# Writing out the order of VectorE and ScalarE through a gated DeltaNet recurrence, with the transposes of each block's normed output behind the next block's products

## The chip, the core and the metric

The kernel runs on one core of one Trainium2 chip (trn2). The metric is device time in microseconds (us), the median over runs. TensorE (PE in the profile) does matmuls and transposes, VectorE (DVE) element-wise work and reductions, ScalarE (ACT) activations, copies and casts, GpSimd (POOL) a few small operations, and SyncE (SP) issues the transfers.

## What is computed

One residual block over 512 tokens of width 1024: a SwiGLU feed-forward half step, a mixer, and a second feed-forward half step, all in float32, each behind an adaptive RMS norm. The change lies in the mixer. Half of it is latent attention; the other half is a gated delta rule with 4 heads of width 128, whose reference carries a state S from chunk to chunk:

```
def step(state, inp):
    u_c, wk_c, qd_c, kd_c, qk_c, gl_c = inp
    v_new = u_c - einsum('bhck,bhkv->bhcv', wk_c, state)
    o_c = einsum('bhck,bhkv->bhcv', qd_c, state) + einsum('bhcs,bhsv->bhcv', qk_c, v_new)
    state = state * gl_c[..., None, None] + einsum('bhck,bhcv->bhkv', kd_c, v_new)
    return state, o_c
...
o_a = _rms(o_a, gdn_norm_w) * silu(gz)
mixed = concatenate([o_a, o_b], axis=-1)       # o_b: the attention's heads
x = x + g2 * (mixed @ w_out)
```

The kernel walks the 512 tokens in four blocks of 128 (p = 0 to 3), so that the recurrence has three steps that depend on a state.

## The kernel before

Float32 products are made of three passes: a tensor is split into a high part, rounded to fp32r, and a low part that holds the rest, and `mm3` (L468 to L470) multiplies high by high, high by low and low by high. The weights come in tiles of 512 KB (`wr`); ScalarE casts the high part (`wh`, L228) and VectorE subtracts for the low part (`wl`, L229). `wr`, `wh` and `wl` have four buffers each, in rotation, so a tile's cast waits until TensorE has used the tile four places ahead of it, and a load waits until the split four places ahead of it is done.

Eight such tiles hold `w_out`: tiles 1 to 4 for the attention's rows, 5 to 8 for the recurrence's rows. `out_attended` multiplies with tiles 1 to 4 (512 columns, L468 to L470); `out_half` multiplies with 5 to 8 for tokens 0 to 255 (256 columns); `out_rest` multiplies with the same tiles for tokens 256 to 511. Each finished output tile is added into `xT` by VectorE (L2391, L2403, L2414), which frees its PSUM buffer; the buffers of `pa` are three in rotation, those of `pb` five.

The recurrence, block p (`recur`): TensorE multiplies the state with `w` (L1966); VectorE subtracts to get `vn` (L1968); TensorE multiplies the state with q (L1974) and ScalarE scales that into `o`; TensorE multiplies `vn` with `kd` for the next state (L1981) and with `qk` for the output (L1989); VectorE makes the new state `S` (L1986) and adds the output into `o` (L1993). GpSimd makes the decayed state `Sg`.

The block's gated norm (`gated_out`): ScalarE squares `o` into `hn` (L2027), VectorE sums it (`gs`, L2028) and makes `ve` (L2003), GpSimd takes the power -1/2 (`ry`, L214), VectorE scales (`on`, L1475), TensorE transposes four 128x128 pieces (L2012), and for each of four heads VectorE makes `mf` (L2018), ScalarE the high part `mh` (L2020) and VectorE the low part `ml` (L2021). `out_half` reads the results of blocks 0 and 1, `out_rest` those of blocks 2 and 3.

Three first weight tiles of the second feed-forward (`fr`, six transfers of 256 KB, split into `fh` and `fl`) are prepared in the same stretch (`early`).

The order. Each engine works off its instructions in program order. The program is written by generators that are stepped in turn: `fill` holds the `w_out` products, `early` the first feed-forward tiles, `gated` the gated norms, `chain` and `rest` what is left of the solving and the attention. A scheduler then places the instructions of all engines by priorities and estimates of its own, unless `follow` ties an instruction behind another one. In the recurrence, `matmuls_in_order` ties TensorE's instructions alone in the order in which they were written (those of `loosely` excepted); VectorE's and ScalarE's order is left to the scheduler.

## Time and profile before

| | |
|---|---|
| three runs | 1026.66, 1027.6, 1026.34 us, median 1026.66 us |
| profiled execution | 1026.66 us, of which the span is 1024.9 us |
| TensorE busy | 1013.4 us, 99% of the span |
| VectorE, ScalarE, GpSimd busy | 775.8, 500.6, 29.4 us |
| weight loads of TensorE (PEld) | 906.2 us |
| granted TensorE clock | 1.0 of full speed |
| moved from and to HBM | 127.18 MB read, 2.49 MB written |
| the stretch of the change | 609 to 644 us of the span |

The profile is one execution. In the rows of a timeline stand the start in us from the span's beginning, the time that the group takes, engine, line, operation, output and inputs, the number of instructions, and in brackets how long the engine idled ahead of it and what ended that. Matmuls are pipelined: a row's length (0.39 us for a 512-column product) is longer than its distance to the next row (0.23 us), and that distance is the price of one more product. On VectorE and ScalarE too a row overlaps the next one by some hundredths.

### The profile page before, as it was taken

To read this page: it belongs to the slowest core of one execution; us is meant where nothing else is said; L and a number is where in the kernel's file an instruction comes from. 1 tells how busy PE (TensorE), PEld (TensorE's weight loads), DVE (VectorE), ACT (ScalarE), POOL (GpSimd) and SP (SyncE) were. 2 spreads that over 40 slices of the span, in tenths; PEclk is the share of its full clock that TensorE was granted. 3 is DMA by queue.
4 is the path that set the end of the run, shared out by engine and by line. 5 is a ranking of instruction groups with operands and counts; after the bars stand their busy time and mean duration, and the time that the engine had idled before them with its cause. 6 is when DMAs were issued, how large, how long until landed. Compare 5 with 4: busy or idle time off the path is not lost.

```text
span 1024.9 us, 16967 instructions
## 1 busy us (share of the span) xinstructions
PE 1013.4 (99%) x6663; PEld 906.2 (88%) x6663; DVE 775.8 (76%) x1363; ACT 500.6 (49%) x895; POOL 29.4 (3%) x74
## 2 busy tenths in 40 slices
PE   8999999999999999999999999999999999999998
PEld 6788899999887899888888888998999999987887
DVE  4789788887787847879888659677888888788541
ACT  5453455556322235567845465364555555634330
POOL 0000000000100000100000011000000000000000
PEclk9999999999999999999999999999999999999999
DMA  9988234344688835311321121122233434383421
GB/s 328 291 271 263 69 98 116 91 123 114 198 290 303 262 83 167 83 42 42 73 73 47 42 83 49 34 58 87 83 108 99 117 90 123 115 274 91 130 61 31
DMA packets 203773, 130.77 MB, mean 128 GB/s; under 512 B 14241, under 2 KB 188334, under 8 KB 203694
## 3 DMA queue, kind: packets, MB, share of 16 engines
q1 hardware_dynamic: 203694, 129.70, 41.9%
q8 instruction: 52, 0.85, 0.3%
q14 instruction: 27, 0.22, 0.1%
HBM read 127.18 MB, written 2.49 MB: 127 GB/s over the span
## 4 chain that ended last, share of the span: by engine, by line
PE 92%; DVE 5%; DMA 1%; issue 1%; ACT 0%; POOL 0%; SPq 0%; DVEq 0%; POOLq 0%
PE pa L354 17%; PE pa L468 16%; PE pa L469 16%; PE pa L470 16%; PE pb L354 13%; PE pa L1250 1%; PE pb L2188 1%; PE pb L2168 1%; PE pb L1250 1%; PE pb L468 1%; PE pb L469 1%; PE pb L470 1%; DVE wl L229 1%; DMA ar<-in_w_ada 1%; PE pb L1743 1%; PE pb L666 1%
## 5 line engine op out<-in xcount | busy, mean ns | idle before, releaser
L228 ACT CAST wh<-wr 128x1024 fp32r<-128x1024 f32 (+1 forms) x93 | 93.8, 1015 | 160.2 <-PE pa L469 130.6
L269 DVE TENSOR_TENSOR wl<-wr,wh 128x1024 fp32r<-128x1024 f32 x96 | 117.3, 1222 | 54.5 <-ACT wh L273 54.5
L229 DVE TENSOR_TENSOR wl<-wr,wh 128x1024 fp32r<-128x1024 f32 (+1 forms) x93 | 108.8, 1176 | 47.2 <-ACT wh L228 46.3
L468 PE MATMUL pa<-hh,wh 128*128 128x512 f32 (+1 forms) x357 | 137.2, 384 | 0.0
L470 PE MATMUL pa<-hh,wl 128*128 128x512 f32 (+1 forms) x357 | 134.9, 378 | 0.0
L469 PE MATMUL pa<-hl,wh 128*128 128x512 f32 (+1 forms) x357 | 134.7, 377 | 0.0
L468 PE MATMUL pa<-ah,wh 128*128 128x512 f32 (+1 forms) x356 | 132.3, 372 | 0.0
L469 PE MATMUL pa<-al,wh 128*128 128x512 f32 (+1 forms) x356 | 131.1, 368 | 0.0
L470 PE MATMUL pa<-ah,wl 128*128 128x512 f32 (+1 forms) x356 | 130.9, 368 | 0.0
L273 ACT CAST wh<-wr 128x1024 fp32r<-128x1024 f32 x96 | 98.0, 1050 | 18.6 <-PE pa L469 11.2
L468 PEld LDWEIGHTS pa<-ah,wh 128*128 128x128 f32 x356 | 67.1, 188 | 13.4 <-ACT wh L228 2.5
L468 PEld LDWEIGHTS pa<-hh,wh 128*128 128x128 f32 x357 | 67.3, 189 | 13.2 <-issue 1.6
L837 DVE SCALAR_TENSOR_TENSOR aa<-ar,sc,aa 128x512 f32<-128x512 f32 x98 | 73.3, 749 | 6.8 <-DMA ar<-in_w_ada 4.8
L470 PEld LDWEIGHTS pa<-hh,wl 128*128 128x128 f32 x357 | 67.3, 188 | 11.9
L470 PEld LDWEIGHTS pa<-ah,wl 128*128 128x128 f32 x356 | 67.1, 188 | 11.0
L469 PEld LDWEIGHTS pa<-hl,wh 128*128 128x128 f32 x357 | 67.4, 189 | 10.7
L469 PEld LDWEIGHTS pa<-al,wh 128*128 128x128 f32 x356 | 67.1, 189 | 10.8
L354 PE MATMUL pa<-hh,wh 128*128 128x256 f32 x240 | 68.0, 283 | 0.0
L354 PE MATMUL pa<-th,wh 128*128 128x256 f32 x240 | 67.9, 283 | 0.0
L354 PE MATMUL pa<-tl,wh 128*128 128x256 f32 x240 | 67.9, 283 | 0.0
L354 PE MATMUL pa<-th,wl 128*128 128x256 f32 x240 | 67.9, 283 | 0.0
L354 PE MATMUL pa<-hh,wl 128*128 128x256 f32 x240 | 67.9, 283 | 0.0
(481 smaller groups left out, 2482.4 us busy)
## 6 DMA issues: line engine op xcount, KB each, us to landing
wr<-in_ffn_w_in SPq DMA_DIRECT2D x79, 512.0 KB
ar<-in_w_ada SPq DMA_DIRECT2D x96, 256.0 KB
wr<-in_ffn_w_out SPq DMA_DIRECT2D x32, 512.0 KB
ar<-in_w_ada SPq DMA_DIRECT2D x22, 512.0 KB
wr<-in_w_in SPq DMA_DIRECT2D x21, 512.0 KB
wr<-in_ffn_w_out SPq DMA_DIRECT2D x16, 384.0 KB
wr<-in_w_out SPq DMA_DIRECT2D x8, 512.0 KB
wr<-in_ffn_w_in SPq DMA_DIRECT2D x8, 384.0 KB
```

Of the source, the lines that this page charges most:

```text
L228: self.nc.scalar.copy(hi, raw)
L229: self.nc.vector.tensor_tensor(out=lo, in0=raw, in1=hi.bitcast(F32), op=ALU.subtract)
L269: sub = lambda out, x, y: nc.vector.tensor_tensor(out=out, in0=x, in1=y, op=ALU.subtract)
L273: nc.scalar.copy(hi[:, :n], raw[:, :n])
L354: nc.tensor.matmul(z, a[:, j, :], b, start=start and j == 0 and i == 0, stop=j == 3 and i == 2, skip_group_check=not start)
L468: mm(out, wh, xh, start=start, stop=False)
L469: mm(out, wh, xl, start=False, stop=False)
L470: mm(out, wl, xh, start=False, stop=stop)
L666: nc.tensor.matmul(pg[32 * q:32 * q + 32, :256], self.sc[:, kc:kc + 1].to_broadcast([P, 32]), a[kc], start=(e == 0), stop=(e == 1), tile_p ...
L837: nc.vector.scalar_tensor_tensor(out=acc, in0=a, scalar=sc, in1=acc, op0=ALU.mult, op1=ALU.add)
L1250: nc.tensor.matmul(z, a[:, j, :], b, start=start and j == 0 and i == 0, stop=j == 3 and i == 2, skip_group_check=not start)
L1743: nc.tensor.matmul(pa[:, ps], kh[:, ps], x[:, ps], start=True, stop=True)
```

## The change

`matmuls_in_order` becomes `steps_in_order`: it ties TensorE's, VectorE's and ScalarE's instructions of the recurrence in the order in which they are written, each engine for itself. Left out are what `loosely` steps (as before) and, on VectorE and ScalarE, the last block's transposing and scaling together with what is left of `fill`.

`gated_out` yields more often: after the squaring, between the transposes and the scaling, and ahead of the low parts; all four `mf` and `mh` stand ahead of the four `ml`. The loop over p steps it by hand: the norm of block p-1 is scaled (`on`) beside the state's products of block p, and its transposes stand straight behind the products with `qk` of block p, where they stood some products later. The sum, `ve` and power of block p stand between block p-1's `mf`, `mh` and its `ml`.

```diff
@@ -162,17 +162,20 @@
             self.ends[i.engine] = i.name
 
     @contextmanager
-    def matmuls_in_order(self, after=None):
-
-        self.loose = set()
+    def steps_in_order(self):
+
+        self.loose, self.free, last = set(), set(), {}
+        engines = mybir.EngineType.PE, mybir.EngineType.DVE, mybir.EngineType.Activation
         with self.traced() as block:
             yield
         for i in block:
-            if i.engine == mybir.EngineType.PE and i.name not in self.loose:
-                if after:
-                    self.follow(i, after)
-                after = i.name
-        self.last_mm = after
+            if i.engine != engines[0] and i.name in self.free:
+                continue
+            if i.engine in engines and i.name not in self.loose:
+                if i.engine in last:
+                    self.follow(i, last[i.engine])
+                last[i.engine] = i.name
+        self.last_mm = last[mybir.EngineType.PE]
 
     @contextmanager
     def queued(self, engine, after=None):
@@ -1998,7 +2001,10 @@
 
         nc = self.nc
         ss = self.small(4, "gs")
-        self.head_squares(self.o[p], ss)
+        sq = self.slot(s="hn")
+        nc.scalar.activation(sq, self.o[p], AF.Square)
+        yield
+        nc.vector.tensor_reduce(out=ss, in_=sq.rearrange("p (h d) -> p h d", h=4), axis=AX.X, op=ALU.add)
         ve = self.small(4, "ve")
         nc.vector.scalar_tensor_tensor(out=ve, in0=ss, scalar=1.0 / P, in1=self.oe[:, 4 * p:4 * p + 4], op0=ALU.mult,
                                        op1=ALU.add)
@@ -2010,16 +2016,19 @@
         pt = self.aux()
         for h in range(4):
             nc.tensor.transpose(pt[:, h * P:(h + 1) * P], on[:, h * P:(h + 1) * P], self.ident)
+        yield
         m = self.slot(s="mf")
         ts = slice(p * P, (p + 1) * P)
-        for h in range(4):
-            hs = slice(h * P, (h + 1) * P)
-            mh, ml = self.mixed[h]
+        parts = [(slice(h * P, (h + 1) * P), *self.mixed[h]) for h in range(4)]
+        for h, (hs, mh, _) in enumerate(parts):
             nc.vector.scalar_tensor_tensor(out=m[:, hs], in0=pt[:, hs], scalar=self.cwT[:, j:j + 1],
                                            in1=self.zT[h][:, ts], op0=ALU.mult, op1=ALU.mult)
             nc.scalar.copy(mh[:, ts], m[:, hs])
+        yield
+        for hs, mh, ml in parts:
             nc.vector.tensor_tensor(out=ml[:, ts], in0=m[:, hs], in1=mh[:, ts].bitcast(F32), op=ALU.subtract)
         self.gated += 1
+        yield
 
     def head_squares(self, o, ss):
 
@@ -2332,43 +2341,59 @@
             self.loose.update(i.name for i in block)
 
         self.mixed[:4] = [(self.slot(F32R, "mh"), self.slot(F32R, "ml")) for _ in range(4)]
-        with self.matmuls_in_order():
-            gated, self.gated = Side(), 0
-
-            def gate(n=1):
-                if gates and not (att.open or att.todo):
-                    gate_silu(4)
-                elif not gates:
-                    gated.step(n)
+        with self.steps_in_order():
+            self.gated = 0
+            outs = []
+
+            def between(n, first=False):
+                loosely(chain, 2)
+                if first:
+                    loosely(rest, 4)
+                else:
+                    early.step()
+                if self.mixed[4] is not None:
+                    fill.step(n)
+
+            def half():
+                while self.gated < 2:
+                    yield
+                yield from self.out_half()
 
             for p in range(NB):
                 while self.wk[p] is None:
                     loosely(chain, 1)
-                for _ in self.recur(p):
-                    loosely(chain, 2)
-                    loosely(rest, 4)
-                    if p:
-                        early.step()
-                    if self.mixed[4] is not None:
-                        fill.step(3)
-                    gate()
-                gated.add(self.gated_out(p))
-                gate()
-                if p == 1:
-                    def half():
-                        while self.gated < 2:
-                            yield
-                        yield from self.out_half()
+                steps = self.recur(p)
+                outs.append(self.gated_out(p))
+                if not p:
+                    next(steps)
+                    next(outs[0])
+                    between(3, True)
+                    while rest.open or rest.todo:
+                        loosely(rest, 1)
+                    gate_silu(4)
+                    next(outs[0])
+                    continue
+                past = outs[p - 1]
+                next(steps)
+                next(past)
+                between(3)
+                next(steps)
+                next(past)
+                next(outs[p])
+                next(past)
+                next(outs[p])
+                next(past)
+                if p == 2:
                     fill.add(half())
-            while rest.open or rest.todo:
-                loosely(rest, 1)
-            gate_silu(4)
+                between(3)
+            next(outs[3])
             early.flush()
-            fill.step(2)
-            gated.step()
-            fill.step(6)
-            gated.flush()
-            fill.flush()
+            fill.step(7)
+            with self.traced() as block:
+                for _ in outs[3]:
+                    pass
+                fill.flush()
+            self.free.update(i.name for i in block)
         with self.in_order({mybir.EngineType.PE: self.last_mm}):
             return self.out_rest()
```

No instruction is added or removed on any engine; 8 rows of TensorE differ in place, some 50 on VectorE, 16 on ScalarE, 2 on GpSimd and 2 on SyncE (the load of `w_out`'s tile 8 stands behind the six loads of `fr` where it stood ahead of them). Lines of the changed kernel lie 3 to 25 higher than those of the one before. Three places follow, first before, then now.

VectorE, from inside block 1's scaling to `vn` of block 3 (`mf`, `ml`: the scaling; `gs`, `ve`: block 2's norm; `wl`: low part of a `w_out` tile, tile 6 before and tile 4 now; `fl`: low part of a feed-forward tile):

```order
L229 TENSOR_TENSOR wl_6926<-wr_6923,wh_6925 128x1024
L2018 SCALAR_TENSOR_TENSOR mf_6770<-pb_6765,cwT_3625,z_5938 128x128
L2018 SCALAR_TENSOR_TENSOR mf_6770<-pb_6765,cwT_3625,z_6075 128x128
L2018 SCALAR_TENSOR_TENSOR mf_6770<-pb_6765,cwT_3625,z_6196 128x128
L2021 TENSOR_TENSOR ml_6532<-mf_6770,mh_6531 128x128
L2021 TENSOR_TENSOR ml_6534<-mf_6770,mh_6533 128x128
L2018 SCALAR_TENSOR_TENSOR mf_6770<-pb_6765,cwT_3625,z_6353 128x128
L2021 TENSOR_TENSOR ml_6536<-mf_6770,mh_6535 128x128
L2028 TENSOR_REDUCE gs_6783<-hn_6784 128x4
L2021 TENSOR_TENSOR ml_6538<-mf_6770,mh_6537 128x128
L2003 SCALAR_TENSOR_TENSOR ve_6787<-gs_6783,oe_5895 128x4
L1968 TENSOR_TENSOR vn_6797<-uu_6572,pb_6792 128x512
```

And now:

```order
L2024 SCALAR_TENSOR_TENSOR mf_6753<-pb_6745,cwT_3625,z_6196 128x128
L2024 SCALAR_TENSOR_TENSOR mf_6753<-pb_6745,cwT_3625,z_6353 128x128
L2007 TENSOR_REDUCE gs_6750<-hn_6751 128x4
L2009 SCALAR_TENSOR_TENSOR ve_6763<-gs_6750,oe_5895 128x4
L2029 TENSOR_TENSOR ml_6532<-mf_6753,mh_6531 128x128
L2029 TENSOR_TENSOR ml_6534<-mf_6753,mh_6533 128x128
L2029 TENSOR_TENSOR ml_6536<-mf_6753,mh_6535 128x128
L2029 TENSOR_TENSOR ml_6538<-mf_6753,mh_6537 128x128
L1474 TENSOR_TENSOR fl_6772<-fr_6360,fh_6771 128x512
L232 TENSOR_TENSOR wl_6778<-wr_6775,wh_6777 128x1024
L1971 TENSOR_TENSOR vn_6797<-uu_6575,pb_6792 128x512
L1478 TENSOR_TENSOR on_6808<-o_6697,ry_6765 128x512
```

Block 2's `gs` and `ve` moved ahead of the four `ml`; the tile split ahead of `vn` is another one, one `fl` moved in, and `on` of block 2 follows `vn` directly.

TensorE, at the end of block 3's products with `qk` (`pa` with `wh`, `wl`: products of `out_attended`; `ident`, `on`: the transposes of block 2):

```order
L1989 MATMUL pb_6821<-vn_6797,qk_5605 128x128
L468 MATMUL pa_6812<-mh_6522,wh_6478 128x512
L469 MATMUL pa_6812<-ml_6523,wh_6478 128x512
L470 MATMUL pa_6812<-mh_6522,wl_6479 128x512
L468 MATMUL pa_6812<-mh_6579,wh_6478 128x512
L469 MATMUL pa_6812<-ml_6580,wh_6478 128x512
L470 MATMUL pa_6812<-mh_6579,wl_6479 128x512
L468 MATMUL pa_6844<-mh_6090,wh_6751 128x512
L469 MATMUL pa_6844<-ml_6091,wh_6751 128x512
L470 MATMUL pa_6844<-mh_6090,wl_6752 128x512
L2012 MATMUL pb_6848<-ident_85,on_6819 128x128 x4
```

And now:

```order
L1992 MATMUL pb_6821<-vn_6797,qk_5605 128x128
L2018 MATMUL pb_6827<-ident_85,on_6808 128x128 x4
L471 MATMUL pa_6814<-mh_6522,wh_6478 128x512
L472 MATMUL pa_6814<-ml_6523,wh_6478 128x512
L473 MATMUL pa_6814<-mh_6522,wl_6479 128x512
L471 MATMUL pa_6814<-mh_6582,wh_6478 128x512
L472 MATMUL pa_6814<-ml_6583,wh_6478 128x512
L473 MATMUL pa_6814<-mh_6582,wl_6479 128x512
```

The transposes moved ahead of nine products of `out_attended`.

ScalarE, from block 1's high parts to block 2's (`hn`: squares; `o`: the scaled product of state and q; `fh`, `wh`: high parts of feed-forward and `w_out` tiles):

```order
L2020 CAST mh_6531<-mf_6770 128x128
L2020 CAST mh_6533<-mf_6770 128x128
L2020 CAST mh_6535<-mf_6770 128x128
L2020 CAST mh_6537<-mf_6770 128x128
L1976 ACTIVATE o_6791<-pb_6799,eG_4793 128x128 x4
L1470 CAST fh_6827<-fr_6363 128x512
L228 CAST wh_6962<-wr_6960 128x1024
L2027 ACTIVATE hn_6867<-o_6791 128x512
L2020 CAST mh_6531<-mf_6853 128x128
L1470 CAST fh_6874<-fr_6364 128x512
```

And now:

```order
L2026 CAST mh_6537<-mf_6753 128x128
L1473 CAST fh_6771<-fr_6360 128x512
L231 CAST wh_6777<-wr_6775 128x1024
L1979 ACTIVATE o_6791<-pb_6799,eG_4793 128x128 x4
L2005 ACTIVATE hn_6833<-o_6791 128x512
L2026 CAST mh_6531<-mf_6835 128x128
L2026 CAST mh_6533<-mf_6835 128x128
L2026 CAST mh_6535<-mf_6835 128x128
L2026 CAST mh_6537<-mf_6835 128x128
L1473 CAST fh_6853<-fr_6363 128x512
L231 CAST wh_6866<-wr_6864 128x1024
L231 CAST wh_6925<-wr_6923 128x1024
```

The squares `hn` now stand ahead of the four `mh`; the casts of tiles 4, 5 and 6 (`wh_6777`, `wh_6866`, `wh_6925`) stand in these rows, where tile 7's (`wh_6962`) stood alone.

## The prediction

> **What bounds the kernel now.** I read the page's first rows, then the busy time by stage, then the timeline of TensorE through the recurrence, then VectorE's, and GpSimd's where VectorE waits for it.

> ```profile
> span 1024.9 us, 16967 instructions
> PE 1013.4 (99%) x6663; PEld 906.2 (88%) x6663; DVE 775.8 (76%) x1363; ACT 500.6 (49%) x895; POOL 29.4 (3%) x74
> ```
> ```profile
> 609.00:644.00 35.00, 32.93 (x202) 28.25 (x201) 28.29 (x62) 19.92 (x45) 6.81 (x6) 1.00 0.15 45
> 674.00:850.00 176.00, 176.00 (x1360) 171.10 (x1360) 143.73 (x216) 97.65 (x170) 0.00 (x0) 1.00 0.34 99
> ```

> TensorE is busy 99% of the span, so only its gaps can be won: 11.5 us in all, 35.00 - 32.93 = 2.07 us of them in the stretch that is rewritten (the columns behind the window are its length, the busy time of PE, PEld, DVE, ACT and POOL, the granted clock, the share of the DMA engines and GB/s). Behind it TensorE is busy 176.00 of 176.00 us: what is won in the recurrence moves what follows forward as it is. One per mille is 1.03 us here; over 0.2% (2.05 us) is about what a measurement of this kernel can tell from no change.

> The gaps, in TensorE's timeline:

> ```profile
> 623.63 0.39 PE L469 MATMUL pa<-ml,wh 128*128 128x512 f32 x1
> 623.85 0.40 PE L470 MATMUL pa<-mh,wl 128*128 128x512 f32 x1
> 624.23 1.16 PE L1981 MATMUL pb<-vn,kd 128*128 128x128 f32 x8
> 625.22 1.06 PE L1989 MATMUL pb<-vn,qk 128*128 128x128 f32 x8
> 626.03 0.48 PE L468 MATMUL pa<-mh,wh 128*128 128x512 f32 x1
> ...
> 632.26 0.39 PE L470 MATMUL pa<-mh,wl 128*128 128x512 f32 x1
> 633.78 1.16 PE L1989 MATMUL pb<-vn,qk 128*128 128x128 f32 x8 [1.12 <-DVE vn L1968]
> 634.69 0.48 PE L468 MATMUL pa<-mh,wh 128*128 128x512 f32 x1
> ...
> 641.87 0.39 PE L470 MATMUL pa<-mh,wl 128*128 128x512 f32 x1
> 643.21 0.66 PE L2012 MATMUL pb<-ident,on 128*128 128x128 f32 x4 [0.95 <-DVE on L1475]
> 643.62 0.36 PE L468 MATMUL pa<-mh,wh 128*128 128x256 f32 x1
> ...
> 644.05 0.28 PE L468 MATMUL pa<-mh,wh 128*128 128x256 f32 x1
> 644.17 0.28 PE L469 MATMUL pa<-ml,wh 128*128 128x256 f32 x1
> ```

> Rows follow each other at 0.22 to 0.23 us for a 512-column product (623.63 to 623.85) and 0.12 us for a 256-column one (644.05 to 644.17). TensorE loses time at three places: for `vn` of block 2 (623.85 to 624.23), for `vn` of block 3 (632.26 to 633.78), and for block 3's `on` (641.87 to 643.21). Why VectorE is late for the second:

> ```profile
> 629.40 1.22 DVE L229 TENSOR_TENSOR wl<-wr,wh 128x1024 fp32r<-128x1024 f32 x1
> 630.53 0.86 DVE L2018 SCALAR_TENSOR_TENSOR mf<-pb,cwT,z 128x128 f32<-128x128 f32 x3
> 631.31 0.48 DVE L2021 TENSOR_TENSOR ml<-mf,mh 128x128 fp32r<-128x128 f32 x2
> 631.72 0.34 DVE L2018 SCALAR_TENSOR_TENSOR mf<-pb,cwT,z 128x128 f32<-128x128 f32 x1
> 631.98 0.28 DVE L2021 TENSOR_TENSOR ml<-mf,mh 128x128 fp32r<-128x128 f32 x1
> 632.17 0.68 DVE L2028 TENSOR_REDUCE gs<-hn 128x4 f32<-128x512 f32 x1
> 632.77 0.28 DVE L2021 TENSOR_TENSOR ml<-mf,mh 128x128 fp32r<-128x128 f32 x1
> 632.97 0.15 DVE L2003 SCALAR_TENSOR_TENSOR ve<-gs,oe 128x4 f32<-128x4 f32 x1
> 633.04 0.68 DVE L1968 TENSOR_TENSOR vn<-uu,pb 128x512 f32<-128x512 f32 x1
> 633.64 0.75 DVE L2403 SCALAR_TENSOR_TENSOR xT<-pa,mod,xT 128x512 f32<-128x512 f32 x1
> 634.31 0.69 DVE L1475 TENSOR_TENSOR on<-o,ry 128x512 f32<-128x512 f32 x1
> ```

> VectorE does not idle here (no row has a bracket), so that `vn` waits for its turn alone: a split, the whole scaling of block 1 and block 2's sum stand ahead of it. The scaling comes that late because its transposes stand behind nine products. The distances are the prices: `wl` 1.13, one `mf` 0.26, one `ml` 0.20, `gs` 0.60, `ve` 0.07, any 128x512 two-input row (`vn`, `S`, `o`, `on`, `fl`) 0.60, `xT` 0.67. For the third gap:

> ```profile
> 640.80 0.15 DVE L2003 SCALAR_TENSOR_TENSOR ve<-gs,oe 128x4 f32<-128x4 f32 x1
> 641.10 1.33 POOL L214 TENSOR_TENSOR ry<-ve,mhalf 128x4 f32<-128x4 f32 x1 [6.82 <-DVE ve L2003]
> 642.46 0.69 DVE L1475 TENSOR_TENSOR on<-o,ry 128x512 f32<-128x512 f32 x1 [0.90 <-POOL ry L214]
> ```

> `ve` of block 3 comes as late as 640.80, then GpSimd's power (1.33 us) and `on` follow one another while TensorE has run out of products.

> **What the three gaps are worth.** First: 0.38 - 0.23 = 0.15, and the products after it take 1.16 where undisturbed ones take 1.06: 0.10. Second: 1.52 - 0.23 = 1.29, and 0.10 again (633.78 to 634.69 is 0.91, against 0.81 from 625.22 to 626.03). Third: 1.34 - 0.23 = 1.11. Together 2.75 us, somewhat over the 2.07 of the busy column, because a pipelined row covers 0.16 us of the gap behind it.

> **What the change leaves of them**, block by block. No instruction is added on any engine; 16 transposes and all products stay, so TensorE's own work costs the same. I take from the written order what VectorE has in line from the moment at which a block's `qk` products are in PSUM, and set it against what TensorE has in line.

> TensorE, from the start of the `qk` products: 0.81, transposes 0.44 (the price 0.41 from 643.21 to 643.62, up to 0.44 where no product follows), nine products 9 x 0.23 + 0.09 = 2.16, the state's two times four products 0.89 (0.99 from 624.23 to 625.22, less the 0.10) + 0.81, nine products 2.16: from their end (0.25 after the next row's start) to the next need of `vn` 6.2 us.

> VectorE to `vn` of block 2: `o` 0.60, four `mf` 1.04, `gs` and `ve` 0.67, four `ml` 0.80, two `xT` 1.34, `vn` until written 0.68: 5.1 us. Cushion 1.1.

> To `vn` of block 3: 0.60 + 1.04 + 0.67 + 0.80 + `fl` 0.60 + `wl` 1.13 + 0.68 = 5.5 us. Cushion 0.7. ScalarE must have cast tile 4 by then: after `o` come `hn`, the last `mh`, `fh` and the cast. VectorE reaches `wl` 3.7 us after the products' end; ScalarE's chain goes through the last `mf` (1.64), one `mh`, `fh` and the cast. The cast takes 1.03 (its row stands below); a half and an eighth of its columns I estimate at 0.6 and 0.3, which makes 3.6. That is level; half a us late would still be covered.

> To `on` of block 3: TensorE has transposes 0.35, six products 1.47 and twenty-four 5.56, less 0.25: 7.1 us. VectorE 0.60 + 1.04 + 0.67 + 0.80 + 0.60 + 0.67 + 1.13 + 0.69 = 6.2. GpSimd's power starts after 2.3 and takes at most 1.4, so it is done 1.8 us before `on` is reached. Cushion 0.9.

> Behind it VectorE stays without a pause: `wl` of tile 6, `fl`, two `xT`, four `mf`, four `ml`, two narrow `xT`, `wl` of tile 7. A narrow `xT` costs 0.40 (the first fence); the second and third have ScalarE's first cast of a second feed-forward tile and SyncE's loads of `w_out` tile 8 and of four feed-forward tiles:

> ```profile
> 646.02 0.48 DVE L2414 SCALAR_TENSOR_TENSOR xT<-pa,mod,xT 128x256 f32<-128x256 f32 x1
> 646.42 0.28 DVE L2021 TENSOR_TENSOR ml<-mf,mh 128x128 fp32r<-128x128 f32 x1
> ```
> ```profile
> 681.98 1.03 ACT L228 CAST wh<-wr 128x1024 fp32r<-128x1024 f32 x1
> ```
> ```profile
> 590.90 0.37 SPq L136 DMA_DIRECT2D wr<-in_w_out  x1
> 623.23 25.59 SPq L136 DMA_DIRECT2D wr<-in_ffn_w_in  x4
> ```

> From the end of block 3's `qk` products to the written low part of tile 7: 6.1 + 1.13 + 0.60 + 1.34 + 1.04 + 0.80 + 0.80 + 1.22 = 13.0 us. TensorE needs it after 7.1 + 0.41 + four tiles of 12 x 0.12 = 1.44 each + 0.24 = 13.5. Cushion 0.5, the thinnest beside ScalarE's.

> Transfers: the load of tile 8 moves from 590.90 to behind the low part of tile 4, at about 631; it is needed, with cast and split, some 17 us later. The four loads of second feed-forward weights (623.23 to 648.8) start up to 16 us later, since the splits that free their buffers do; their first cast is at 681.98. Both lie under cover unless a load takes over 16 us; at the stretch's mean rate of 45 GB/s, with everything else that it carried, 512 KB take 11.7. The first feed-forward loads move ahead, at no cost.

> The written order itself makes an instruction wait whose engine could have done another. Its price no row shows; the cushions bound it from one side (nothing), and VectorE's idle in the stretch, 35.00 - 28.29 = 6.7 us, spent wholly behind written waits, from the other. I take nothing, since each cushion is positive by rows of the same shapes.

> **Sum.** -2.75 us in the profiled execution, which took 1026.66 us (span 1024.9), the median of the three runs (1026.34 to 1027.6). 1026.66 - 2.75 = 1023.9.

> **Rivals.** *VectorE becomes late.* In the new order it works 13.0 us without a pause against 13.5. If one wait like the 0.90 for GpSimd's power falls into that line, tile 7's low part comes 0.4 late, and the wait passes on to tile 8's; two such, with ScalarE's cast of tile 4 late too, cost 0.7 to 1.8. For it: cushions of 0.5 and about nothing. Against: the power has 1.8 us to spare. Some 1025.0.

> *The gaps stay.* A split still stands ahead of `vn` of block 3. If ScalarE reaches tile 4's cast 2 us late, behind `hn`, four `mh` and `fh`, TensorE waits 1.3 us for `vn` as before, and the line behind is late as well: 1026.7. Against it: ScalarE is busy 19.92 of 35 us.

> *Slower: tile 8's load.* Its transfer now waits for tile 4's split. The gain is gone when it lands 19 us after its issue instead of the 11.7 at the mean rate, and 0.2% more when after 21; at 22 us TensorE waits 5 us at tile 8: about 1029. For it: SyncE's queue is in order, and the wait is new. Against: nothing else is being loaded then, as the loads behind it wait for later splits.

> *More is won than the gaps.* TensorE's weight loads are busy 28.25 of 35.00 us; if the other 6.75 were waits, a better order could win them: 1019.9. [...] The trace speaks against it here: the products run row on row at 0.22 us from 623.63 to 623.85 with nothing to wait for, where a load takes 28.25 / 201 = 0.14 us in the mean; a share of 81% is what unhindered products show, so the distances between rows decide.

> **Chances.** The gaps go and nothing replaces them: 0.57, 1023.9, its own range 1023.0 to 1024.7 (a cushion missed by 0.5, the spread of the three runs below it). VectorE late: 0.25. Gaps stay: 0.09. Slower: 0.05. More won: 0.04. The bound of 0.2% lies at 1024.6, close to the likeliest time: faster 0.53 + 0.04 + 0.02 of the late cases = 0.59; within 0.2% 0.04 + 0.23 + 0.09 = 0.36; slower 0.05. Range 1023.0 to 1026.7: it holds all but the slower and the larger gain, and reaches to the kept gaps.

> **What would show it.** Right: in the changed kernel the rows with `vn` and `on` carry no idle bracket on TensorE, the first 256-column product starts at about 640.9 instead of 643.62, and `gs` of a block starts right behind the four `mf`. Wrong: a bracket on a `w_out` product that waits for `wl` or `xT` (VectorE late), on the `qk` products (gaps stay), or ScalarE's last `w_out` cast waiting for a transfer (slower). If the recurrence ends 2.7 us earlier and the span does not, something behind it was bound by another engine, against the 176.00 of 176.00.

## The result and the profile after

The changed kernel takes 1023.76 us (median of nine runs, 1023.26 to 1025.33), the one before 1026.81 us on the same chip (nine runs, 1026.34 to 1027.6): a ratio of 0.9973, 95% interval 0.9964 to 0.9982. The forecast was 1023.9 us, with a range of 1023.0 to 1026.7. The profiled execution took 1023.66 us, span 1021.6.

The page's busy times and the busy time by stage, changed kernel (columns as before: length, PE, PEld, DVE, ACT, POOL, clock, share of the DMA engines, GB/s):

```profile
PE 1012.0 (99%) x6663; PEld 906.0 (89%) x6663; DVE 775.7 (76%) x1363; ACT 500.3 (49%) x895; POOL 28.9 (3%) x74
```
```profile
609.00:644.00 35.00, 35.00 (x227) 31.49 (x226) 30.25 (x69) 20.57 (x48) 6.28 (x6) 1.00 0.15 44
674.00:850.00 176.00, 175.99 (x1360) 171.09 (x1360) 145.16 (x216) 97.78 (x173) 0.00 (x0) 1.00 0.35 99
```

TensorE is busy 35.00 of 35.00 us where it had 32.93. Its timeline at the three places:

```profile
623.39 0.40 PE L473 MATMUL pa<-mh,wl 128*128 128x512 f32 x1
623.62 1.05 PE L1984 MATMUL pb<-vn,kd 128*128 128x128 f32 x8
...
631.53 0.39 PE L473 MATMUL pa<-mh,wl 128*128 128x512 f32 x1
631.76 1.05 PE L1992 MATMUL pb<-vn,qk 128*128 128x128 f32 x8
632.65 0.60 PE L2018 MATMUL pb<-ident,on 128*128 128x128 f32 x4
...
639.71 0.40 PE L473 MATMUL pa<-mh,wl 128*128 128x512 f32 x1
639.94 0.60 PE L2018 MATMUL pb<-ident,on 128*128 128x128 f32 x4
640.30 0.36 PE L471 MATMUL pa<-mh,wh 128*128 128x256 f32 x1
```

The rows behind `vn` and `on` have no bracket; each starts 0.23 us after the row ahead of it, the price of a product. VectorE's line ahead of `vn` of block 3:

```profile
626.21 1.12 DVE L2024 SCALAR_TENSOR_TENSOR mf<-pb,cwT,z 128x128 f32<-128x128 f32 x4
627.24 0.68 DVE L2007 TENSOR_REDUCE gs<-hn 128x4 f32<-128x512 f32 x1
627.96 0.16 DVE L2009 SCALAR_TENSOR_TENSOR ve<-gs,oe 128x4 f32<-128x4 f32 x1
628.03 0.89 DVE L2029 TENSOR_TENSOR ml<-mf,mh 128x128 fp32r<-128x128 f32 x4
628.84 0.68 DVE L1474 TENSOR_TENSOR fl<-fr,fh 128x512 fp32r<-128x512 f32 x1
629.45 1.22 DVE L232 TENSOR_TENSOR wl<-wr,wh 128x1024 fp32r<-128x1024 f32 x1
630.58 0.68 DVE L1971 TENSOR_TENSOR vn<-uu,pb 128x512 f32<-128x512 f32 x1
```

`vn` is written at 631.26, 0.50 ahead of its use at 631.76. `gs` stands right behind the four `mf`, as foretold.

Two distances within one trace compare kernels more sharply than the medians. D runs from the start of block 1's `qk` products to the first 256-column product; E from the same point to the mixer's last product with `w_out`. Before: 616.82, 643.62, 667.93, so D 26.80 and E 51.11. After: 616.33, 640.30, 664.60, so D 23.97 and E 48.27. D shrank by 2.83, E by 2.84. The other 0.5 us between the spans (1024.9 and 1021.6) arose ahead of the changed stretch: block 1's `qk` products already start 0.49 earlier, and the traces lie as far apart at 592 us (592.60 and 592.11 for the same product), in work that the change leaves alone. So only 2.84 us are the change's. Where below a median and a distance differ by a few tenths, the distance is the finer measure.

### The profile page after: what moved, and what is told of

Its sections match the earlier page's. It is cut to its first block, busy times and chain, and to the rows that moved or that the text cites. A ratio compares the mean times of both kernels' runs of the same rounds, so it can differ in the third digit from the quotient of the medians.

```text
span 1021.6 us, 16977 instructions
## 1 busy us (share of the span) xinstructions
PE 1012.0 (99%) x6663; PEld 906.0 (89%) x6663; DVE 775.7 (76%) x1363; ACT 500.3 (49%) x895; POOL 28.9 (3%) x74
## 4 chain that ended last, share of the span: by engine, by line
PE 95%; DVE 3%; DMA 1%; ACT 0%; issue 0%; SPq 0%; POOL 0%; DVEq 0%
PE pa L357 17%; PE pa L471 17%; PE pa L472 16%; PE pa L473 16%; PE pb L357 13%; PE pa L1253 1%; PE pb L2197 1%; PE pb L2177 1%; PE pb L1253 1%; PE pb L471 1%; PE pb L472 1%; PE pb L473 1%; PE pb L1746 1%; PE pb L669 1%; DVE cv L1690 1%; DMA vecs<-in_b_ada 1%
## 5 line engine op out<-in xcount | busy, mean ns | idle before, releaser
L471 PEld LDWEIGHTS pa<-ah,wh 128*128 128x128 f32 x356 | 67.1, 188 | 13.5 <-ACT wh L231 2.5
L272 DVE TENSOR_TENSOR wr<-wr,wr 128x512 f32<-128x512 f32 x96 | 66.4, 691 | 2.1
```

The lines of the kernel that those rows point to most:

```text
L272: sub = lambda out, x, y: nc.vector.tensor_tensor(out=out, in0=x, in1=y, op=ALU.subtract)
L471: mm(out, wh, xh, start=start, stop=False)
```

## Experiments: which part of the change wins

| kernel | median us | ratio to before (95%) | D | E |
|---|---|---|---|---|
| before | 1026.3 to 1026.8 | | 26.80 | 51.11 |
| changed | 1023.76 | 0.9973 (0.9964 to 0.9982) | 23.97 | 48.27 |
| TensorE alone tied | 1024.14 | 0.9979 (0.9971 to 0.9988) | 24.72 | 49.03 |
| TensorE and ScalarE tied | 1024.34 | 0.9983 (0.9973 to 0.9992) | 23.97 | 48.93 |
| TensorE and VectorE tied | 1025.27 | 0.9991 (0.9982 to 1.0) | 26.10 | 50.40 |
| early sum undone | 1023.78 | 0.9970 (0.9959 to 0.9982) | 23.97 | 48.27 |
| transposes late again | 1029.38 | 1.0030 (1.0020 to 1.0039) | 29.04 | 54.39 |
| order of before, tied | 1037.70 | 1.0102 (1.0087 to 1.0118) | 33.05 | 62.17 |

**TensorE alone tied.**

```diff
-            if i.engine in engines and i.name not in self.loose:
+            if i.engine == engines[0] and i.name not in self.loose:
```

> The changed kernel with TensorE's instructions alone tied in the written order; VectorE's and ScalarE's order is left to the scheduler again. Its order on VectorE: ahead of vn of block 3 stand o, the low part of tile 5, four mf, gs, ml, ve, three ml, fl (the same content as in the changed kernel, 4.8 us, the split first instead of last); ahead of block 3's on stands the low part of tile 6. My theory (the gain is three gaps of TensorE, and they go because the transposes and with them the scaling come nine products earlier): the gaps go here as well, the distance from the end of block 1's qk products to the first 256-column product stays at 23.1 us within 0.2 (25.99 before, 23.07 in the changed kernel), and the time is 1023.8, 0.3 either way. Rival (the written order of VectorE and ScalarE is what wins): the scheduler's order brings gaps back, the distance is 24 to 26 us and the time 1025 to 1026.7.

D grew by 0.75: the early transposes bring 2.08 of the 2.84 us (E), not all of it. TensorE waits again for `vn` of block 3, and the cause lies a block earlier. VectorE's and GpSimd's timelines of this kernel:

```profile
618.50 1.44 DVE L2416 SCALAR_TENSOR_TENSOR xT<-pa,mod,xT 128x512 f32<-128x512 f32 x2 [0.38 <-PE pa L473]
619.85 1.12 DVE L2024 SCALAR_TENSOR_TENSOR mf<-pb,cwT,z 128x128 f32<-128x128 f32 x4
...
621.68 0.16 DVE L2009 SCALAR_TENSOR_TENSOR ve<-gs,oe 128x4 f32<-128x4 f32 x1
...
623.34 1.52 DVE L1478 TENSOR_TENSOR on<-o,ry 128x512 f32<-128x512 f32 x1 [0.30 <-POOL ry L217]
```
```profile
621.91 1.39 POOL L217 TENSOR_TENSOR ry<-ve,mhalf 128x4 f32<-128x4 f32 x1 [10.48 <-DVE ve L2009]
623.28 1.03 POOL L1478 TENSOR_TENSOR Sg<-S,gl 128x512 f32<-128x512 f32 x1
```

The scheduler puts two `xT` ahead of block 1's `mf`, where the written order has them behind `ml`. So `ve` comes at 621.68 instead of 619.78, `on` waits 0.30 for the power, and then takes 1.52 instead of 0.68 while GpSimd's `Sg` (623.28 to 624.31) runs beside it. These 1.1 us go on to `vn` of block 3.

**One more engine tied.** The same line with `engines[:2]` (VectorE), then with `engines[::2]` (ScalarE):

> The changed kernel with TensorE and VectorE tied and ScalarE's order left to the scheduler. With TensorE alone tied, 0.75 us of the gain was missing: VectorE did two xT ahead of block 1's scaling, so that the sum, GpSimd's power and on came about 1 us late and on then stood behind GpSimd's Sg. If it is VectorE's written order that wins those 0.75 us: from the start of block 1's qk products to the first 256-column product 23.97 us as in the changed kernel, 0.1 either way (26.80 before, 24.72 with TensorE alone tied), the time 1023.8. If it is ScalarE's order: 24.4 to 24.8, 1024.3.

> The changed kernel with TensorE and ScalarE tied and VectorE's order left to the scheduler. Its VectorE puts the split of tile 6 behind block 3's ml instead of ahead of them. To the first 256-column product 23.97 us, 0.1 either way, as VectorE's content ahead of every vn and on is the same. But the low part of tile 6 is then written at about 644.2 and TensorE needs it at 640.3 + 2 x 1.44 + 0.24 + 0.1 = 643.5: a wait of 0.7 for wl and 0.1 of restart in the products with tiles 5 to 8; time 1024.5. Rival (that split has room): no wait, 1023.8.

The first is a miss, and the larger one: VectorE's order without ScalarE's leaves a gap of 1.60 us for `vn` of block 3 (D 26.10, with 0.20 more ahead of the state's products and three restarts of 0.10; a restart is what the products behind a wait take longer). The scheduler lets ScalarE cast a `w_out` tile early, ahead of `o` and `fh`, and that cast waits for TensorE to free its buffer; VectorE, tied, waits behind it for `fh`, with `xT`, `S` and `o` in line behind. ScalarE's and VectorE's timelines:

```profile
623.32 1.05 ACT L231 CAST wh<-wr 128x1024 fp32r<-128x1024 f32 x1 [2.89 <-PE pa L472]
624.27 1.14 ACT L1979 ACTIVATE o<-pb,eG 128x128 f32<-128x128 f32 x4
625.28 0.63 ACT L1473 CAST fh<-fr 128x512 fp32r<-128x512 f32 x1
```
```profile
625.94 0.69 DVE L1474 TENSOR_TENSOR fl<-fr,fh 128x512 fp32r<-128x512 f32 x1 [2.04 <-ACT fh L1473]
```

The second came as expected: D 23.97, and then the wait for the low part of tile 6 (0.57, with 0.10 of restart, where 0.7 and 0.1 were expected):

```profile
643.08 0.28 PE L472 MATMUL pa<-ml,wh 128*128 128x256 f32 x1
643.77 0.38 PE L473 MATMUL pa<-mh,wl 128*128 128x256 f32 x1 [0.41 <-DVE wl L232]
```

So the gaps need ScalarE's order beside the early transposes, and VectorE's order adds tile 6's split ahead of block 3's scaling. VectorE's order without ScalarE's costs more than it brings. What an engine does when it is left free is the choice of this scheduler, so the sizes hold for it alone.

**The early sum undone.**

```diff
-                next(outs[p])
                 next(past)
+                next(outs[p])
```

> The changed kernel with one part undone: the sum gs, ve and with them GpSimd's power stand behind the four ml instead of between mf and ml. VectorE's content ahead of every vn and on is the same; ve comes 0.80 us later, so that the power, done 1.8 us before block 3's on is reached by my working, is done about 1.0 before. Expected: no gap, the distance 23.1 within 0.1, the time 1023.8, 0.2 either way. Rival (the early sum is what keeps the power off the path): on waits for GpSimd, a gap of up to 0.8, 1024.5.

As expected: 23.97 and 48.27 again. `gs` and `ve` between `mf` and `ml` win nothing here; GpSimd's power has room.

**The transposes late again**, the written order kept:

```diff
                 next(steps)
-                next(past)
                 next(outs[p])
-                next(past)
-                next(outs[p])
-                next(past)
                 if p == 2:
                     fill.add(half())
                 between(3)
+                next(past)
+                next(past)
+                next(outs[p])
+                next(past)
```

> The changed kernel with all three engines still tied, but the transposes put back behind the nine products that follow the qk products, as before the change, and the scaling with them. Worked out from the rows: from the end of block 2's qk products the transposes are done after 2.16 + 0.44 + 0.25 = 2.85 us, then four mf 1.04, gs and ve 0.67, four ml 0.80, vn 0.68: 6.0 against the need at 6.2, since fl and the split of tile 4 now stand ahead of the mf, in the time in which VectorE would wait for the transposes. So vn of block 3 is just in time (gap 0 to 0.3). For block 3's on: 2.85 + 1.04 + gs 0.60 + a split 1.13 + ve 0.07 + power 1.4 + on 0.69 = 7.8 against 7.1: gap 0.7. Sum 0.7 to 1.2 us over the changed kernel: 1024.5 to 1025.0, the distance 23.8 to 24.3. If the place of the transposes were the whole of it, all three gaps would be back: 1026.5 and 26 us. If the written order of VectorE were the whole of it, nothing would come back: 1023.8 and 23.1.

Slower than before, against all three expectations. VectorE's timeline:

```profile
627.54 0.68 DVE L1996 TENSOR_TENSOR o<-o,pb 128x512 f32<-128x512 f32 x1
629.48 0.69 DVE L1474 TENSOR_TENSOR fl<-fr,fh 128x512 fp32r<-128x512 f32 x1 [1.26 <-ACT fh L1473]
630.43 1.23 DVE L232 TENSOR_TENSOR wl<-wr,wh 128x1024 fp32r<-128x1024 f32 x1 [0.25 <-ACT wh L231]
631.57 1.12 DVE L2024 SCALAR_TENSOR_TENSOR mf<-pb,cwT,z 128x128 f32<-128x128 f32 x4
```

The working counted `fl` and the split as filling the time until the transposes, but left out that ScalarE makes their high parts behind `hn`, which needs this block's `o`. Two written waits, 1.26 and 0.25, and an `o` that starts 0.7 later than assumed (627.54, the `qk` products done at 626.82) put `mf` at 631.57; the transposes were there at 629.3. So `vn` of block 3 is 1.91 us late, and block 3's `on` 2.62. That is the price of a written order which the prediction could only bound. In the changed kernel `fl` and the split stand behind the scaling, when their high parts are ready.

The gaps explain 4.6 of the 6.12 us by which E grew over the changed kernel. The rest is the clock; the busy time in steps of 3 us from the second gap on (the granted clock stands behind POOL's busy time):

```profile
643.00:646.00 3.00, 0.54 (x3) 0.12 (x2) 2.10 (x8) 1.56 (x2) 1.53 (x1) 0.93 0.65 194
646.00:649.00 3.00, 3.00 (x15) 3.00 (x16) 3.00 (x5) 0.00 (x0) 0.00 (x0) 0.50 0.41 122
649.00:652.00 3.00, 3.00 (x27) 3.00 (x27) 2.50 (x10) 1.88 (x6) 0.00 (x0) 1.00 0.33 98
```

For 3.1 us after the gap, until 648.98, TensorE runs at a granted clock of 0.50: 256-column rows are 0.21 us apart instead of 0.12, some 1.5 us lost.

**The order of before, tied.**

```diff
-        with self.matmuls_in_order():
+        with self.steps_in_order():
```

(`steps_in_order` itself is the function of the change.)

> The kernel before with one thing of the change alone: VectorE's and ScalarE's instructions are tied in the order in which the program of before is written, with mf and ml of a head in turn, the transposes behind nine products, and the splits of tiles 6 to 8 behind block 3's scaling. My theory: tying as such wins nothing. In this order each ml waits for ScalarE's mh of its own head, about 0.87 us for a pair, 3.5 us for four; vn comes 2.85 + 3.5 + 0.67 + 0.68 = 7.7 us after the qk products against 6.2, so 1.5 us of gap at vn of blocks 2 and 3, and 2.0 at block 3's on (9.1 against 7.1); the splits of tiles 6 to 8 then come late as well, 1 to 3 us more. Slower than before: 1028.5 to 1031, the distance 28 to 29 us. Rival (tying is the gain, whatever order is written): as fast as the changed kernel, 1023.8.

The direction was right, the size too small: E is 11.06 over the kernel before, 13.90 over the changed one. `mf` and `ml` in turn take 0.92 a pair, since each `ml` waits for ScalarE's `mh`. Of the 13.90 us, gaps of 1.93, 2.07 and 3.22 at the three places make 7.2, two stretches at half clock some 3.0, and waits for tiles 6 to 8 with their restarts 3.3. This kernel also ties the last block's scaling and what is left of `fill`, which the change leaves free, so the 3.3 cannot be put down to the old order alone. Tying wins nothing by itself.

## Experiments: how much slack is left, and what a gap costs

Copies were added on VectorE, one, three, six or eight ahead of `vn` of block 3,

```diff
+            if last:
+                x = self.slot(s="x")
+                for _ in range(3):
+                    nc.vector.tensor_copy(x, self.us[p])
             vn = self.slot(s="vn")
```

or one or three in the same way behind block 2's `ml`. One copy moves VectorE by 0.34 us (its row to the next), three by 1.26, so each further one by 0.46, where 0.6 was expected; six and eight 2.64 and 3.56.

> The changed kernel with one 128x512 copy more on VectorE, put right ahead of vn of block 3 (its result is not used). In the changed kernel vn of block 3 is written at 631.26 and TensorE takes it up at 631.76: cushion 0.50. At 0.6 us for the copy, TensorE waits about 0.1 and the time is 1023.9; if a copy takes less than 0.5, nothing is seen. Rival (VectorE's line has no slack, each us of VectorE counts): 0.6 later, 1024.4.

> The same with three copies ahead of vn of block 3. Cushion theory: TensorE waits for three copies less 0.50, so 1.3 us at 0.6 us a copy, in one idle bracket on block 3's kd or qk products that names vn; the distance to the first 256-column product grows from 23.07 by 1.3, and the time is 1025.1. It is the second gap of the kernel before, made again by as much VectorE work as the change had taken from ahead of vn. Rival (TensorE's line is moved by something else): no bracket, no growth. Rival without slack: 1.8 us.

> The changed kernel with one 128x512 copy more on VectorE behind block 2's four ml, ahead of fl, xT, a split and block 3's on. From there VectorE runs without a pause to the low part of tile 7. In the changed kernel block 3's on is written 0.70 ahead of its use and the low part of tile 7 at 646.05 against a need at 646.3 to 646.5. At 0.6 a copy: no wait at on (0.1 left), 0.1 to 0.35 at tile 7's third product, the time 1024.0. Rival (the thinnest cushion is at on): a wait ahead of the transposes and none at tile 7.

> The same with three copies. At 0.6 a copy, 1.8 us: TensorE waits 1.1 for block 3's on (1.8 less the cushion 0.70), and 0.2 to 0.5 more at tile 7's low part (1.8 less 0.25 to 0.45 less the 1.1 by which TensorE is late by then). Together 1.3 to 1.6: the time 1025.2. Rival (only the thinnest cushion counts once): a wait of 1.4 in one place. Rival without slack: 1.8 us, 1025.6.

| kernel | VectorE later by | median us | ratio (95%) | D | E |
|---|---|---|---|---|---|
| `vn`, one copy | 0.34 | 1023.55 | 0.9971 (0.9960 to 0.9982) | 23.95 | 48.26 |
| `vn`, three | 1.26 | 1024.38 | 0.9982 (0.9973 to 0.9991) | 24.86 | 49.19 |
| behind `ml`, one | 0.34 | 1024.24 | 0.9981 (0.9971 to 0.9990) | 23.97 | 48.59 |
| behind `ml`, three | 1.26 | 1024.58 | 0.9982 (0.9972 to 0.9991) | 24.63 | 49.52 |
| `vn`, six | 2.64 | 1026.99 | 1.0006 (0.9997 to 1.0015) | 26.21 | 50.52 |
| `vn`, eight | 3.56 | 1028.29 | 1.0023 (1.0013 to 1.0034) | 27.14 | 51.46 |

The cushion ahead of `vn` behaves as read: 0.34 us are swallowed, of 1.26 us 0.81 come through, with 0.10 of restart. TensorE's timeline with three copies:

```profile
631.78 0.39 PE L473 MATMUL pa<-mh,wl 128*128 128x512 f32 x1
632.82 1.16 PE L1996 MATMUL pb<-vn,qk 128*128 128x128 f32 x8 [0.65 <-DVE vn L1975]
```

Behind `ml` the sizes are right and the place is not. One copy costs 0.32 us, but at the thirteenth 256-column product (641.71), 4.7 us ahead of the one that takes the low part of tile 7 (646.37); three copies show the name:

```profile
640.22 0.66 PE L2018 MATMUL pb<-ident,on 128*128 128x128 f32 x4 [0.46 <-DVE on L1478]
...
642.62 0.39 PE L471 MATMUL pa<-mh,wh 128*128 128x256 f32 x1 [0.31 <-DVE xT L2432]
```

The second output tile of `out_half` needs a `pa` buffer, which an `xT` of the last 512-column products frees. Worked out from one copy, that cushion is 0.34 + 0.10 - 0.32 = 0.12 us; it is the thinnest. The prediction named a wait for `xT` as a sign of being wrong, but gave it no cushion. With three copies `on` is 0.56 late (1.26 less 0.70) and the buffer 0.47 more, each with 0.10 of restart: 1.23 against 1.25 in E.

Larger doses ask what a gap costs beyond its length.

> The changed kernel with six copies ahead of vn of block 3, 0.34 + 5 x 0.46 = 2.64 us by the rows of the kernels with one and three copies. Less the cushion of 0.45 TensorE waits 2.2 us in one place. Two theories on the price of a gap. Linear: 2.2 + 0.1, to the first 256-column product 26.3 us, time 1026. Clock: in the two kernels that were slower than expected the rows behind a gap of 2.07 and of 2.62 us ran at a granted clock of 0.50 for some 3.3 us, behind 1.91 and 1.93 at 1.00; then the rows behind this gap take twice as long for 3.3 us as well, 1.65 us more: 27.9 us, time 1027.5, so slower than the kernel before although its gaps together are smaller.

> The same with eight copies, 3.56 us; TensorE waits 3.1 us. Linear: 3.2 us over the changed kernel, 27.2 us to the first 256-column product, time 1027. Clock: one stretch of some 3.3 us at half speed on top, 28.8 us and 1028.5; if the length of the slow stretch follows the length of the gap, 29 or more.

Both theories hold, for different executions. In the profiled ones D is 26.21 and 27.14, linear to 0.1, with the clock at 1.00 behind gaps of 2.16 and 3.09 us. With eight copies, around the gap from 631.47 to 634.40 and behind it:

```profile
629.54:632.95 3.41, 1.94 (x9) 1.24 (x7) 3.20 (x8) 1.03 (x4) 0.00 (x0) 1.00 0.45 150
632.95:636.36 3.41, 1.96 (x15) 1.88 (x16) 3.32 (x7) 0.00 (x0) 0.00 (x0) 1.00 0.01 4
636.36:639.78 3.42, 3.42 (x17) 2.79 (x16) 3.39 (x12) 3.40 (x8) 1.13 (x1) 1.00 0.00 0
```

Over all runs the mean granted clock parts them: with six copies five runs at 0.999 to 1.000 took 1025.64 to 1026.64 us and five at 0.997 to 0.998 took 1027.34 to 1029.27; with eight, three at 1.000 took 1026.18 to 1026.61 and seven at 0.996 to 0.998 took 1027.84 to 1031.76. One stretch of 3.4 us at half speed is 0.5 x 3.4 / 1026 = 0.0017 of the mean. No run of the kernels whose gaps stay at 1.6 us or below had less than 0.999. So in these kernels a gap of about 2 us or more cost half speed for some 3 us on top in some executions and not in others; the last section shows what that went with. That the runs at the lowest means had a second or third such stretch is likely from the number alone; no profile shows it, nor why they would.

## Why the prediction was right

- **The sum.** All three gaps went: 0.15 + 0.10, 1.29 + 0.10 and 1.11 us. D shows 2.83 instead of 2.75. Of the 0.08, 0.05 is a restart that the sum left out at the third gap: the transposes behind it were 0.41 us from the next row (643.21 to 643.62), now they are 0.36 (639.94 to 640.30). The rest is spread over many rows in hundredths.
- **The time.** That 1023.9 and the median of 1023.76 lie 0.14 apart is in part luck: the nine runs spread from 1023.26 to 1025.33, and the medians differ by 3.05 where the change made 2.84.
- **First 256-column product** at 640.30, foretold at 640.9: 0.49 of it is the earlier start, and 0.08 the difference above.
- **Cushions**, foretold and measured: `vn` of block 2 1.1 and 0.94; `vn` of block 3 0.7 and 0.50; block 3's `on` 0.9 and 0.70; tile 7's low part 0.5 and 0.3. GpSimd's power was done 1.86 ahead of `on` (1.8). ScalarE's cast of tile 4 ended 0.18 ahead of VectorE's split, "level" as foretold. VectorE's four are some 0.2 us thinner than worked out, about 0.1 of it at `gs`, where `ve` follows after 0.72 (627.24 to 627.96) and not 0.60. The thinnest, the `pa` buffer at 0.12, was missing: the list went by operands and left out the buffers that a tile writes to.
- **VectorE late** (chance 0.25) did not come, but one copy of 0.34 us was enough to make it come (0.32 us, at the `pa` buffer).
- **Gaps stay** (0.09): not in this kernel; with ScalarE's order free it is what happened (1.60 us at `vn` of block 3). The rival named ScalarE's cast behind `hn`, `mh` and `fh`; the one that hurts is a cast too early, ahead of `fh`.
- **Slower through tile 8's load** (0.05): the load was issued at 630.69, foretold 631; the last cast waits for TensorE, not for a transfer:

```profile
639.91 1.05 ACT L231 CAST wh<-wr 128x1024 fp32r<-128x1024 f32 x1 [0.90 <-PE pa L472]
```

- **More than the gaps** (0.04): no. With TensorE without a gap its weight loads are busy 31.49 of 35.00 us, and in its 512-column products from 633.4 to 639.7 only 5.18 of 6.30, with nothing to wait for. So the 1.12 us without a weight load there are nothing that a better order could win.
- **What the written order costs** was taken as nothing, between nothing and 6.7 us. It is nothing in the changed kernel, and 1.9 and 2.6 us of gap in two places with late transposes. The value was right because ScalarE's order was written along with VectorE's and the transposes stand early; the prediction named neither as a condition.

## What to carry to other kernels

Tie an engine's order only together with that of the engine that feeds it, and place each step where its operand is ready: with the early transposes, tying all three engines won 2.84 us, TensorE alone 2.08 and TensorE with VectorE 0.71; tying the old order lost 11. List a cushion for buffers as well as for operands, in us, and test it with a small dose of work on the engine in question. A TensorE gap of up to 1.93 us cost its length and 0.1 here; from 2.07 us on it cost half speed for some 3 us more in some executions (the mean clock was down in 5 of 10 with six copies, in 7 of 10 with eight).

## What the runs showed of the hardware

The granted clock fell to 0.50 behind gaps of 2.07, 2.62 and 3.22 us, and not behind 1.91, 1.93, 2.16 and 3.09 (each in one execution), so the length alone does not decide. The moments at which it changed lie whole multiples of 3.41 us apart: with the order of before tied, it fell at 636.42, rose at 639.84, fell at 650.08 and rose at 653.49 (differences 3.41, 10.24 and 3.41); in the kernel before it was full from 10.35 to 1024.11 us, in the changed one from 8.06 to 1021.81, 1013.76 us in both, which is 297 times 3.4133. Read in windows of 3.41 us between such moments, how long TensorE idled in one went with the clock of the next. Three windows of the kernel with the order of before tied:

```profile
622.77:626.18 3.41, 1.64 (x10) 1.12 (x9) 2.72 (x7) 2.96 (x9) 1.01 (x1) 1.00 0.00 0
633.01:636.42 3.41, 1.51 (x9) 0.99 (x8) 2.77 (x7) 2.86 (x8) 0.97 (x1) 1.00 0.12 40
636.42:639.83 3.41, 3.41 (x13) 2.93 (x12) 2.05 (x4) 0.45 (x1) 0.03 (x1) 0.50 0.00 0
```

The record of the full clock starts at 10.35 us in the kernel before and at 8.06 in the changed one, 2.29 apart, so I take it as chance where a gap falls in the windows. An estimate from these figures: if any place is as likely as another, a single idle stretch g leaves more than a limit T in one window in (3.41 + g - 2T) / 3.41 of the executions. With T from 1.77 to 1.90 that is 0.47 to 0.55 for six copies (g 2.00) and 0.74 to 0.82 for eight (g 2.92); the mean clock was down in 5 and 7 of 10 runs.

Twice a row of VectorE's `on` took longer beside GpSimd's `Sg`, 1.52 us with TensorE alone tied (the rows shown above) and 1.30 with late transposes, against 0.68 in the changed kernel. With late transposes, VectorE's row and then GpSimd's:

```profile
624.46 1.30 DVE L1478 TENSOR_TENSOR on<-o,ry 128x512 f32<-128x512 f32 x1
```
```profile
624.17 1.04 POOL L1478 TENSOR_TENSOR Sg<-S,gl 128x512 f32<-128x512 f32 x1
```

In both kernels `on` ends 0.55 us after `Sg` (624.31 to 624.86, 625.21 to 625.76), nearly its own 0.60, as if it had started only then. In the changed kernel `Sg` ends at 622.04 and `on` starts at 622.60, 0.56 us apart.
